# A decoder layer on one core: v's two parts side by side, a mask by select, the embedding's projection inside the mixer, and a new written order

## The chip, the cores and the metric

The kernel runs on 1 core of one Trainium2 chip. The metric is the device time in microseconds (us) of one launch. The engines are PE (TensorE), DVE (VectorE), ACT (ScalarE), POOL (GpSimd) and SP (SyncE, which here issues the transfers). Each takes its instructions strictly in the order in which they were emitted.

## The reference

One decoder layer on x of 512 tokens and 1024 features, in float32:

```python
x = x + 0.5 * swiglu(rmsnorm(x, g1), wgu1, wdown1)          # 1024 -> 2 x 2816 -> 1024
h = rmsnorm(x, g_mix);  z = h @ w_in                        # zq, zk, zv, zc, zg
q, k = rope(rmsnorm(zq)), rope(rmsnorm(zk)); v = zv         # 16 query heads, 2 key heads, 64 wide
a = attention(q, k, v, sinks, window=128, block=128) @ attn_proj
ca, cb = split(zc); u = ca * sigmoid(cb)
c = silu(layernorm(causal_depthwise_conv31(u))) @ conv_proj
ga, gb = split(zg)
x = x + (sigmoid(ga) * a + sigmoid(gb) * c) @ w_out
x = x + 0.5 * swiglu(rmsnorm(x, g2), wgu2, wdown2)
e = rmsnorm(p @ ple_proj, g_ple)                            # p: 512 x 256
x = x + sigmoid(rmsnorm(x, g_gate) @ ple_gate_w) * e
```

A query sees the 128 latest keys, itself included: of the block before it those later than its own place, of its own block those not later.

## The kernel before, in words

Features lie on the 128 partitions and the 512 tokens are the columns, so nearly every product is one of 128x128 by 128x512 into one PSUM bank. Float32 accuracy comes from three products of a reduced type per tile (`mm3`, line 691): a value is split into a high part (a copy by ACT) and a low part (a subtraction by DVE, or by POOL where the name is in `FLEX`), `split_into` (line 664), and high x low, high x high and low x high are added up in PSUM. A weight piece of 128x1024 is loaded and split in the same way, `piece` (line 679): tiles `raw_`, `whi_`, `wlo_`, three buffers each. Other tiles of 128x512 share 53 buffers.

The parts follow each other: the first feed-forward part (`ffn`, line 840: products f_g and f_u for each of 22 columns of the hidden layer, then f_d), the mixer, cp (conv_proj), wo (w_out), the second feed-forward part, the embedding's projection e, the gate pg and the output. In `ffn` the norm is applied behind the product, so products start on x times the gain (h_h, h_l) while the sum of squares (n_sq) is still being made.

The string `ORDER` (line 40) lists the mixer's steps by letter and number: K keys and values, Q queries of one key head group, a and b the convolution's two inputs (products ca, cb), A scores (transposes qTp, products sc), E softmax, V values (`values`, line 1113: transposes pT, products o), g and h the two gates (products ga, gb), p the attention's projection (ap), L the layer norm (ln_). For A, E and V the numbers 0 to 3 are the four blocks of 128 tokens of head group 0, 4 to 7 those of group 1. Channels 0, 2 and 4 of the convolution run on POOL (taps y<-y,ct), the other five on DVE (cz, 31 taps each).

In `values`, for each block of tokens but the first, o of a head group is the sum over both key heads hh of (v of the block before) x (softmax weights p) + (dv, v of this block less that before) x (the weights po, with keys later than the query set to zero by a product with a mask). Both heads go into one bank: the stationary operand is v with 64 zero columns, so that each head reaches its own half of the rows, and each of the 2 or 4 terms takes three products.

`record` writes all steps down as instructions, `simulate` (line 384) places them in time by a table of costs and of free buffers, with `deadlines` (line 357) as priorities, and `hybrid_layer` (line 1288) emits every engine's instructions in the order of the starts found (all through line 1314, hence one line number in every row). PE takes groups of products in the written order, and may take one of the next 8 groups when the first isn't ready.

Of the kernel before, what the change touches and what calls it, by code (L numbers as in the profile page):

```python
# [16 lines left out]
P = 128  # L17
# [5 lines left out]
KF = FF // P  # L23
# [17 lines left out]
K0 a0 a1 Q0 b1 a2 b2 b0 A0 a3 A1 b3 E0 E1 A2 a4 V0 E2 A3 a5 E3 V1 b4 Q1 V2 V3  # L41
b5 A4 g5 a6 A5 E4 A6 V4 E5 a7 b7 A7 g4 V5 g3 h4 E6 V6 E7 g6 g2 V7 b6 g1 g0 p0
p2 L0 h6 h7 g7 h1 p1 p7 h3 p5 p3 h2 p6 h0 p4 h5
"""
POOLCH = (0, 2, 4)
WARM = 9
FLEX = ("wkv", "wq", "wzc", "wzg", "wap")
# [3 lines left out]
class VT:  # L51


    def __init__(self, name, shape, dtype, cls):
        self.name, self.shape, self.dtype, self.cls = name, tuple(shape), dtype, cls
        self.log = []
        self.left = 0
        self.slot = self.real = None
        self.late = False

# [159 lines left out]
class Program:  # L220
# [65 lines left out]
    def costs(self, op, eng=None):  # L286
# [9 lines left out]
        vecs = sum(isinstance(v, V) for v in list(op.a[3:]) + list(op.k.values()))  # L296
# [24 lines left out]
        elif eng == "ACT":  # L321
            op.cost, op.lat = 0.07 + n * 0.88e-3, 0.17
            if vecs:
                op.cost += 0.08
# [32 lines left out]
def deadlines(prog, when):  # L357
# [5 lines left out]
    for op in reversed(prog.ops):  # L363
# [9 lines left out]
        for s in op.succs:  # L373
            d = s.ls
            if s.preds[op] and not s.eng == op.eng == "PE":
                d -= op.lat + (1.8 + op.dma if op.eng == "SP" else 0.0)
            ls = min(ls, d - op.cost)
        op.ls = ls
# [5 lines left out]
def simulate(prog, slots):  # L384

    free = {c: deque(range(n)) for c, n in slots.items()}
    cap = {"cz": 2}
    ncz = 0
# [24 lines left out]
    for op in prog.ops:  # L413
        if op.npred == 0:
            push(0.0, "ready", op)
    push(0.0, "wake")
# [6 lines left out]
    def can(op, slack):  # L423
# [10 lines left out]
        for c, vts in need.items():  # L434
# [7 lines left out]
            if any(vt.name.startswith("cz") for vt in vts) and ncz >= cap["cz"]:  # L442
# [3 lines left out]
    def launch(op, t):  # L446
        nonlocal dma_free, aset, ncz, lock_dve, lock_pool
        for v in op.writes:
            vt = v.vt
            if vt.slot is None:  # L450
                vt.slot = free[vt.cls].popleft()
                if vt.name.startswith("cz"):
                    ncz += 1
# [80 lines left out]
    while left:  # L534
# [4 lines left out]
        while events and events[0][0] <= t + 1e-9:  # L539
            _, _, kind, x = heapq.heappop(events)  # L540
            if kind == "done":
# [8 lines left out]
                for vt in x.vts:  # L550
                    vt.n -= 1
                    if vt.n == 0:
                        free[vt.cls].append(vt.slot)
                        if vt.name.startswith("cz"):
                            ncz -= 1
            elif kind == "ready" and x.eng != "PE":
                insort(ready[x.eng], (x.ls, x.i, x))
        for e in ENGINES:
# [11 lines left out]
            for key, _, op in ready[e]:  # L570
                if best is not None and key >= best[0]:
                    break
                if e == "ACT" and op.fset and op.fset != aset:
# [61 lines left out]
def record():  # L635
# [165 lines left out]
    for k in range(KD):  # L801
        sq = ftile(f"n1_sq{k}")
        nc.scalar.activation(sq, x[k], AF.Square)
# [7 lines left out]
    masks = nc.tile("masks", [P, 2, W], F32, "c")  # L811
# [28 lines left out]
    def ffn(tag, wgu, wdown, h, ss, after, cuts, late):  # L840
# [18 lines left out]

        for i in range(KF):  # L860
            ws = [piece(wgu, 2 * i + kh, cuts=cuts if i == 0 else 1) for kh in range(2)]
            pg, pu = ps_tile(f"{tag}_g{i}"), ps_tile(f"{tag}_u{i}")
            if i == late and late:
                rb = spread(f"{tag}_n", r)
            kn = 2 if i == late else KD
            for k0 in range(0, KD, kn):
                with nc.group(f"{tag}_gu{i}_{k0}"):
                    for k in range(k0, k0 + kn):
                        c = (k % 4) * 256
                        for j, ps in enumerate((pg, pu)):  # L870
                            mm3(
                                ps, part(ws[k // 4], slice(c + j * P, c + (j + 1) * P)), h[k], k == 0, k == KD - 1,
                                0 if cuts > 1 and i == k == 0 else 1,
                            )
# [29 lines left out]
    ffn("f1", "wgu1", "wd1", h, ss, after, 4, 2)  # L904
# [93 lines left out]
    kz = [nc.tile(f"kz{p}", [P, NT, 2, P], F32R, "k") for p in "hl"]  # L998
    for z in kz:
        nc.gpsimd.memset(z.bitcast(F32)[HD:P, :, 0], 0.0)  # L1000
        nc.gpsimd.memset(z.bitcast(F32)[0:HD, :, 1], 0.0)

    vp = [nc.tile(f"v{t}", [P, 2, 3, HD], F32R, "a") for t in range(NT)]

    dv = [nc.tile(f"dv{t}", [P, 2, 3, HD], F32R, "a") if t else None for t in range(NT)]
    vf = nc.tile("vf", [P, NT, NKV, HD], F32, "a")

    def keys_values():
# [3 lines left out]
        for t in range(NT):  # L1012
# [4 lines left out]
            nc.gpsimd.memset(vp[t].bitcast(F32)[:, :, 1], 0.0)  # L1017
# [396 lines left out]
```

## Time and profile before

| | us |
|---|---|
| median of 3 runs (lowest, highest) | 1218.81 (1218.6, 1219.24) |
| the profiled execution | 1218.67 |
| its span in the profile | 1216.8 |
| PE busy | 1201.5 (99%) |
| DVE, ACT, POOL busy | 732.6, 490.2, 332.7 |

PE is the engine that is always at work. The chain of work that ended last lies on PE for 90% of the span. A matmul's row shows 0.39 us, but the products overlap: what one costs is the distance from its start to the next start. "[3.42 <-DVE oT1l L1314]" behind a row says that the engine was idle for 3.42 us before it and that the last thing it waited for was oT1l on DVE. Names in rows of the trace have their numbers taken off: f_g is that of any column.

### The profile page before, as it was taken

To read this page: it belongs to the slowest core of one execution; us is meant where nothing else is said; L and a number is where in the kernel's file an instruction comes from. 1 tells how busy PE (TensorE), PEld (TensorE's weight loads), DVE (VectorE), ACT (ScalarE), POOL (GpSimd) and SP (SyncE) were. 2 spreads that over 40 slices of the span, in tenths; PEclk is the share of its full clock that TensorE was granted. 3 is DMA by queue.
4 is the path that set the end of the run, shared out by engine and by line. 5 is a ranking of instruction groups with operands and counts; after the bars stand their busy time and mean duration, and the time that the engine had idled before them with its cause. 6 is when DMAs were issued, how large, how long until landed. Compare 5 with 4: busy or idle time off the path is not lost.

```text
span 1216.8 us, 14137 instructions
## 1 busy us (share of the span) xinstructions
PE 1201.5 (99%) x5408; PEld 996.7 (82%) x5408; DVE 732.6 (60%) x1019; ACT 490.2 (40%) x780; POOL 332.7 (27%) x345
## 2 busy tenths in 40 slices
PE   9999999999999999998999999999999999999998
PEld 7888888888888887877888888888888888888886
DVE  5644445434446888997898775755444444344466
ACT  5433223222223749769573463333233232222251
POOL 2000000001112798996897200510000000022230
PEclk9999999999999999999999999999999999999999
DMA  7232222333332231212122323232322323333321
GB/s 239 87 104 89 102 99 92 100 91 99 96 100 90 86 103 53 72 51 70 64 91 89 101 91 113 95 104 87 104 91 100 101 90 100 92 98 97 100 87 70
DMA packets 35203, 115.11 MB, mean 95 GB/s; under 512 B 4416, under 2 KB 6080, under 8 KB 35136
## 3 DMA queue, kind: packets, MB, share of 16 engines
q1 hardware_dynamic: 34992, 114.18, 28.9%
q8 instruction: 42, 0.69, 0.2%
q14 instruction: 25, 0.20, 0.1%
q10 hardware_dynamic: 144, 0.03, 0.0%
HBM read 112.10 MB, written 2.10 MB: 94 GB/s over the span
## 4 chain that ended last, share of the span: by engine, by line
PE 90%; ACT 5%; DVE 3%; issue 1%; DMA 0%; SPq 0%; DVEq 0%
PE f_d L1314 20%; PE f_g L1314 19%; PE f_u L1314 19%; PE pg L1314 4%; PE ap L1314 4%; PE wo L1314 4%; PE cp L1314 4%; PE gb L1314 3%; ACT s L1314 3%; PE ga L1314 3%; PE ca L1314 3%; PE cb L1314 3%; PE q0b L1314 2%; DVE cz L1314 1%; PE kvb L1314 1%; PE e L1314 1%
## 5 line engine op out<-in xcount | busy, mean ns | idle before, releaser
L1314 ACT ACTIVATE whi_wgu<-raw_wgu 128x1024 fp32r<-128x1024 f32 (+1 forms) x94 | 94.5, 1005 | 254.3 <-PE f_u L1314 233.4
L1314 DVE TENSOR_TENSOR wlo_wgu<-raw_wgu,whi_wgu 128x1024 fp32r<-128x1024 f32 (+1 forms) x94 | 110.3, 1175 | 108.3 <-ACT whi_wgu L1314 108.3
L1314 DVE TENSOR_TENSOR wlo_wd<-raw_wd,whi_wd 128x1024 fp32r<-128x1024 f32 (+1 forms) x48 | 65.7, 1369 | 102.2 <-ACT whi_wd L1314 102.2
L1314 ACT ACTIVATE whi_wd<-raw_wd 128x1024 fp32r<-128x1024 f32 (+1 forms) x48 | 47.5, 990 | 177.1 <-PE f_d L1314 107.6
L1314 POOL TENSOR_TENSOR y<-y,ct 128x511 f32<-128x511 f32 (+28 forms) x90 | 113.8, 1285 | 4.8 <-DVE y L1314 3.0
L1314 POOL TENSOR_TENSOR pg_ss_sq<-x 128x512 f32<-128x512 f32 x8 | 8.3, 1039 | 338.1 <-DVE x L1314 324.1
L1314 DVE SCALAR_TENSOR_TENSOR cz<-u,dww,cz 128x504 f32<-128x504 f32 (+24 forms) x145 | 100.0, 728 | 0.8
L1314 POOL TENSOR_TENSOR mix_ss_sq<-x 128x512 f32<-128x512 f32 x8 | 8.3, 1040 | 328.7 <-DVE x L1314 328.7
L1314 PE MATMUL f_d<-f_a_h,wlo_wd 128*128 128x512 f32 x224 | 87.1, 389 | 0.0
L1314 PE MATMUL f_d<-f_a_h,whi_wd 128*128 128x512 f32 x224 | 87.1, 389 | 0.0
L1314 PE MATMUL f_d<-f_a_l,whi_wd 128*128 128x512 f32 x224 | 87.1, 389 | 0.0
L1314 DVE TENSOR_TENSOR f_gs<-f_g,f_n_rb 128x512 f32<-128x512 f32 x44 | 30.3, 691 | 94.1 <-PE f_g L1314 92.6
L1314 PE MATMUL f_g<-h_h,wlo_wgu 128*128 128x512 f32 x176 | 69.0, 392 | 1.0 <-DVE wlo_wgu L1314 0.9
L1314 PE MATMUL f_g<-h_h,whi_wgu 128*128 128x512 f32 x176 | 68.9, 391 | 0.0
L1314 PE MATMUL f_g<-h_l,whi_wgu 128*128 128x512 f32 x176 | 68.6, 390 | 0.0
L1314 PE MATMUL f_g<-f_h_h,wlo_wgu 128*128 128x512 f32 x176 | 68.6, 390 | 0.0
L1314 PE MATMUL f_u<-h_h,wlo_wgu 128*128 128x512 f32 x176 | 68.5, 389 | 0.0
L1314 PE MATMUL f_u<-h_h,whi_wgu 128*128 128x512 f32 x176 | 68.5, 389 | 0.0
L1314 PE MATMUL f_g<-f_h_l,whi_wgu 128*128 128x512 f32 x176 | 68.5, 389 | 0.0
L1314 PE MATMUL f_u<-f_h_h,wlo_wgu 128*128 128x512 f32 x176 | 68.5, 389 | 0.0
L1314 PE MATMUL f_g<-f_h_h,whi_wgu 128*128 128x512 f32 x176 | 68.5, 389 | 0.0
L1314 PE MATMUL f_u<-h_l,whi_wgu 128*128 128x512 f32 x176 | 68.5, 389 | 0.0
(407 smaller groups left out, 3163.2 us busy)
## 6 DMA issues: line engine op xcount, KB each, us to landing
raw_wgu<-in_wgu SPq DMA_DIRECT2D x86, 512.0 KB, 3.5
raw_wd<-in_wd SPq DMA_DIRECT2D x32, 512.0 KB, 3.5
raw_wzc<-in_wzc SPq DMA_DIRECT2D x16, 512.0 KB, 3.5
raw_wzg<-in_wzg SPq DMA_DIRECT2D x16, 512.0 KB, 3.5
raw_wd<-in_wd SPq DMA_DIRECT2D x16, 384.0 KB, 3.1
raw_wq<-in_wq SPq DMA_DIRECT2D x8, 512.0 KB, 3.4
raw_wap<-in_wap SPq DMA_DIRECT2D x8, 512.0 KB, 3.5
raw_wcp<-in_wcp SPq DMA_DIRECT2D x8, 512.0 KB, 3.5
```

Of the source, the lines that this page charges most:

```text
L1314: getattr(engines[op.eng], op.what)(*a, **k)
```

## The change

1. `values`: the stationary operand is [v_hi | v_lo], 64 columns each, so one product gives both halves of p_h x v. Each term takes two products (p_h, p_l) and each head has a bank of its own; ACT copies the half that came from the low part to SBUF (`of`) and DVE adds the two halves.
2. The weights of the own block come from a select on POOL (`affine_select`) on p_h and p_l instead of a product with a mask on DVE or POOL.
3. The squares for the norms of queries and keys move from POOL to ACT. kz is laid out by head; seven memsets of v and dv go, and their splits are made for each head apart.
4. The embedding's projection (8 x 6 products, its norm) is a step "e" of the mixer. Its eight results are kept through the second feed-forward part.
5. `ffn`: the first two columns of the first part are computed side by side (loop over the 8 feature tiles outside, over the two columns inside), with the weights of both in four cuts. The squares for its norm start no earlier than 14.0 on the planner's clock. In the second part the first column is one group of 48 products rather than four.
6. The planner: a limit of four `ct` tiles, another price of vector operands on ACT, and a new `ORDER`.

```diff
 ORDER = """
-K0 a0 a1 Q0 b1 a2 b2 b0 A0 a3 A1 b3 E0 E1 A2 a4 V0 E2 A3 a5 E3 V1 b4 Q1 V2 V3
...
+K0 a0 a2 a1 Q0 A0 b2 b1 b0 a3 A1 E0 E1 b3 A2 E2 a4 V0 A3 a5 E3 V1 b4 Q1 V2 b5
...
+g1 p0 p2 g7 L0 p3 p6 p4 h3 p7 p5 p1 e0 h5 h6 e1 h0 h2
 """
...
+        sq.vt.after = 14.0
         nc.scalar.activation(sq, x[k], AF.Square)
...
-    masks = nc.tile("masks", [P, 2, W], F32, "c")
+    masks = nc.tile("masks", [P, W], F32, "c")
...
+        def products(i, ks):
+            if i not in gu:
+                gu[i] = ps_tile(f"{tag}_g{i}"), ps_tile(f"{tag}_u{i}")
+            for k in ks:
+                if k % 4 == 0:
+                    ws[i] = piece(wgu, 2 * i + k // 4, cuts=cuts if i < late else 1)
...
+                for j, ps in enumerate(gu[i]):
+                    mm3(
+                        ps, part(ws[i], slice(c + j * P, c + (j + 1) * P)), h[k], k == 0, k == KD - 1,
+                        0 if cuts > 1 and i == k == 0 else 1,
+                    )
+        for k in range(KD if late else 0):
+            for i in range(late):
+                products(i, [k])
         for i in range(KF):
-            ws = [piece(wgu, 2 * i + kh, cuts=cuts if i == 0 else 1) for kh in range(2)]
...
-            nc.gpsimd.tensor_tensor(sq, z3, z3, op=ALU.mult)
+            nc.scalar.activation(sq, z3, AF.Square)
...
             for o, p in zip(po, pr):
-                nc.flex.tensor_tensor(
-                    o.rearrange("p (j k) -> p j k", j=4), p.bitcast(F32).rearrange("p (j k) -> p j k", j=4), own,
-                    op=ALU.mult,
+                nc.gpsimd.affine_select(
+                    o, p.bitcast(F32), pattern=[[0, 4], [1, W]], compare_op=ALU.is_ge, fill=0.0,
+                    base=0, channel_multiplier=-1,
                 )
             parts.append((hh, dv[t], po))
-        po = ps_tile(f"o{g}_{t}")
-        with nc.group(f"o{g}_{t}"):
-            for n, (hh, v, pr) in enumerate(parts):
-                vv = [v[:, i, hh : hh + 2].rearrange("p a d -> p (a d)") for i in range(2)]
-                mm3(po, vv, pr, n == 0, n == len(parts) - 1)
+        of = ftile(f"of{g}_{t}")
+        for hh in range(2):
+            po = ps_tile(f"o{g}_{t}_{hh}")
+            mine = [(v, pr) for h, v, pr in parts if h == hh]
+            with nc.group(f"o{g}_{t}_{hh}"):
+                for n, (v, pr) in enumerate(mine):
+                    vv = v[:, hh].rearrange("p a d -> p (a d)")
+                    nc.tensor.matmul(po, vv, pr[0], start=n == 0, stop=False)
+                    nc.tensor.matmul(po, vv, pr[1], start=False, stop=n == len(mine) - 1)
+            r, other = (slice(h * HD, (h + 1) * HD) for h in (hh, 1 - hh))
+            nc.scalar.copy(of[r], po[other])
+            nc.vector.tensor_tensor(of[r], po[r], of[r], op=ALU.add)
         to = [o[:, :, t * P : (t + 1) * P] for o in oq[g]]
-        split_into(to[0], to[1], po.rearrange("p (j k) -> p j k", j=4))
+        split_into(to[0], to[1], of.rearrange("p (j k) -> p j k", j=4))
...
+    def embedding(i):
...
+        w = piece("wple", i)
+        for j in range(4):
...
+                    mm3(ps, part(w, slice(c, c + P)), pin[k], k == 0, k == KP - 1)
+            e = ftile(f"es{n}")
+            nc.scalar.copy(e, ps)
+            es.append(e)
+            sse.add(ps, on_act=True)
+        if len(es) == KD:
+            rbe = spread("ple", mean_rstd("ple", sse.accs, D))
```

Three places show how the instructions stand. First, SP at the program's start, before and then after; raw_wgu10 is the first weight piece of column 0, raw_wgu12 that of column 1, x0 to x3 are tiles of the input.

```order
L1314 DMA x0_70<-in_xT 128x512
L1314 DMA raw_wgu10_78<-in_wgu1 128x256
L1314 DMA x1_83<-in_xT 128x512
L1314 DMA raw_wgu10_78<-in_wgu1 128x256
L1314 DMA x2_98<-in_xT 128x512
L1314 DMA raw_wgu10_78<-in_wgu1 128x256
L1314 DMA x3_104<-in_xT 128x512
L1314 DMA raw_wgu10_78<-in_wgu1 128x256
L1314 DMA x4_112<-in_xT 128x512
```

```order
L1346 DMA x0_70<-in_xT 128x512
L1346 DMA raw_wgu10_78<-in_wgu1 128x256
L1346 DMA raw_wgu12_83<-in_wgu1 128x256
L1346 DMA x1_89<-in_xT 128x512
L1346 DMA raw_wgu10_78<-in_wgu1 128x256
L1346 DMA raw_wgu12_83<-in_wgu1 128x256
L1346 DMA x2_104<-in_xT 128x512
L1346 DMA raw_wgu10_78<-in_wgu1 128x256
L1346 DMA raw_wgu12_83<-in_wgu1 128x256
```

Between two tiles of x there is now a cut of column 1 beside that of column 0.

Second, PE where the scores of head group 1 begin, before and then after; sc1_1_3 is the last score product of block 1 of that group, qTp1_2 the transposes of the queries of block 2, ga5 an attention gate.

```order
L1314 MATMUL sc1_0_3_4262<-kzh_72,qT1_0_l_4199 128x256
L1314 MATMUL sc1_0_3_4262<-kzh_72,qT1_0_h_4184 128x256
L1314 MATMUL sc1_0_3_4262<-kzl_101,qT1_0_h_4184 128x256
L1314 MATMUL qTp1_1_4272<-ident_74,zq1_1_4053 128x128 x4
L1314 MATMUL qTp1_2_4289<-ident_74,zq1_2_4061 128x128 x4
L1314 MATMUL sc1_1_0_4307<-kzh_72,qT1_1_l_4300 128x512
L1314 MATMUL sc1_1_0_4307<-kzh_72,qT1_1_h_4284 128x512
L1314 MATMUL sc1_1_0_4307<-kzl_101,qT1_1_h_4284 128x512
```

```order
L1346 MATMUL sc1_1_3_4308<-kzh_72,qT1_1_l_4199 128x512
L1346 MATMUL sc1_1_3_4308<-kzh_72,qT1_1_h_4184 128x512
L1346 MATMUL sc1_1_3_4308<-kzl_101,qT1_1_h_4184 128x512
L1346 MATMUL qTp1_2_4317<-ident_74,zq1_2_4115 128x128 x4
L1346 MATMUL ga5_4323<-mix_h0_h_1946,wlo_wzg10_4207 128x512
L1346 MATMUL ga5_4323<-mix_h0_h_1946,whi_wzg10_4190 128x512
L1346 MATMUL ga5_4323<-mix_h0_l_1966,whi_wzg10_4190 128x512
```

Before, the transposes of two blocks and the scores that read them stand behind each other. After, a gate's 24 products stand behind the transposes of block 2.

Third, PE around the transposes of the softmax weights of group 1, before and then after; pT1_1_0 belongs to block 1 and key head 0, o1_2_0 is the values' product of block 2 and key head 0, cb6 the convolution's gate of channel 6.

```order
L1314 MATMUL pT1_1_0_4750<-ident_74,s1_1_0_4316 128x128 x2
L1314 MATMUL pT1_1_0_4750<-ident_74,s1_1_1_4334 128x128 x2
L1314 MATMUL pT1_1_1_4759<-ident_74,s1_1_0_4316 128x128 x2
L1314 MATMUL pT1_1_1_4759<-ident_74,s1_1_1_4334 128x128 x2
L1314 MATMUL pT1_2_0_4766<-ident_74,s1_2_0_4354 128x128 x2
L1314 MATMUL pT1_2_0_4766<-ident_74,s1_2_1_4370 128x128 x2
L1314 MATMUL pT1_2_1_4774<-ident_74,s1_2_0_4354 128x128 x2
L1314 MATMUL pT1_2_1_4774<-ident_74,s1_2_1_4370 128x128 x2
L1314 MATMUL ga6_4787<-mix_h0_h_1940,wlo_wzg12_4684 128x512
```

```order
L1346 MATMUL o1_2_0_4712<-p1_2_0_h_4656,v1_2772 128x512
L1346 MATMUL o1_2_0_4712<-p1_2_0_l_4666,v1_2772 128x512
L1346 MATMUL o1_2_0_4712<-po1_2_0h_4683,v2_2779 128x512
L1346 MATMUL o1_2_0_4712<-po1_2_0l_4692,v2_2779 128x512
L1346 MATMUL pT1_1_0_4726<-ident_74,s1_1_0_4290 128x128 x2
L1346 MATMUL pT1_1_0_4726<-ident_74,s1_1_1_4312 128x128 x2
L1346 MATMUL cb6_4734<-mix_h0_h_1946,wlo_wzc13_4660 128x512
L1346 MATMUL cb6_4734<-mix_h0_h_1946,whi_wzc13_4644 128x512
L1346 MATMUL cb6_4734<-mix_h0_l_1966,whi_wzc13_4644 128x512
```

Before, the transposes of two blocks stand together ahead of ga6. After, two of them at a time stand between products of the convolution's inputs and of the values.

## Rows read from the trace of the kernel before

**Rows 1.** The first part of the page: the span, and of each engine the busy time, its share of the span and its instructions.

```profile
span 1216.8 us, 14137 instructions
PE 1201.5 (99%) x5408; PEld 996.7 (82%) x5408; DVE 732.6 (60%) x1019; ACT 490.2 (40%) x780; POOL 332.7 (27%) x345
```

**Rows 2.** The timeline of PE in the first up-projections, one row per product of 128x512: start, duration, engine, line, operation and tiles; the rows left out are 41 more products.

```profile
19.64 0.39 PE L1314 MATMUL f_u<-h_l,whi_wgu 128*128 128x512 f32 x1
...
29.16 0.39 PE L1314 MATMUL f_u<-h_l,whi_wgu 128*128 128x512 f32 x1
```

**Rows 3.** The view of the waits of PE over the span, by the tile that waited and the one waited for: us in total, times, longest.

```profile
PE ga L1314 <- DVE oT1l L1314: 3.4, 1, 3.4
PE sc L1314 <- DVE qT_l L1314: 1.6, 1, 1.6
PE qTp L1314 <- DVE s L1314: 1.1, 1, 1.1
PE f_g L1314 <- DVE wlo_wgu L1314: 0.9, 1, 0.9
```

**Rows 4.** The view by windows of 20 us: the window, its length, then PE, PEld, DVE, ACT and POOL busy with their instructions, PE's granted clock, the DMA share and GB/s.

```profile
460.00:480.00 20.00, 19.23 (x94) 15.68 (x94) 16.59 (x32) 19.99 (x71) 16.30 (x29) 1.00 0.08 27
...
520.00:540.00 20.00, 17.24 (x86) 14.27 (x85) 19.72 (x36) 12.75 (x24) 19.27 (x25) 1.00 0.16 53
...
560.00:580.00 20.00, 16.57 (x80) 13.69 (x79) 15.79 (x30) 19.97 (x67) 12.64 (x26) 0.90 0.24 75
580.00:600.00 20.00, 20.00 (x88) 16.50 (x87) 16.75 (x25) 11.13 (x20) 15.98 (x15) 0.93 0.17 56
...
640.00:660.00 20.00, 20.00 (x90) 16.57 (x89) 19.97 (x30) 6.04 (x9) 18.73 (x14) 1.00 0.23 79
```

**Rows 5.** The timeline of PE around the longest wait.

```profile
571.76 1.94 PE L1314 MATMUL pT<-ident,s 128*128 128x128 f32 x16
577.12 0.79 PE L1314 MATMUL ga<-mix_h_h,wlo_wzg 128*128 128x512 f32 x1 [3.42 <-DVE oT1l L1314]
577.71 0.63 PE L1314 MATMUL ga<-mix_h_h,whi_wzg 128*128 128x512 f32 x1
...
582.41 0.58 PE L1314 MATMUL ga<-mix_h_h,wlo_wzg 128*128 128x512 f32 x1
```

**Rows 6.** The timeline of PE and ACT at the start; the product at 8.20 is the seventh, that at 19.64 in Rows 2 the 54th.

```profile
3.42 0.63 ACT L1314 ACTIVATE n_sq<-x 128x512 f32<-128x512 f32 x1 [0.97 <-DMA x<-in_xT]
5.02 0.79 PE L1314 MATMUL f_g<-h_h,whi_wgu 128*128 128x512 f32 x1
...
6.30 0.73 ACT L1314 ACTIVATE h_h<-x,g_all 128x512 fp32r<-128x512 f32 x1 [1.34 <-DMA x<-in_xT]
...
8.20 0.50 PE L1314 MATMUL f_g<-h_h,wlo_wgu 128*128 128x512 f32 x1 [0.92 <-DVE wlo_wgu L1314]
```

**Rows 7.** The groups of PE by line and form, the values' product of v and the high part of the weights: busy us, mean ns of one, idle before.

```profile
L1314 PE MATMUL o<-p_h,v 128*128 128x512 f32 x32 | 9.9, 392 | 0.0
```

**Rows 8.** The groups of DVE by line and form: the low half of a weight piece in the feed-forward parts and in attn_proj, a mask product of values(), a low half of the attention output, a convolution tap.

```profile
L1314 DVE TENSOR_TENSOR wlo_wgu<-raw_wgu,whi_wgu 128x1024 fp32r<-128x1024 f32 x86 | 107.1, 1245 | 108.3 <-ACT whi_wgu L1314 108.3
L1314 DVE TENSOR_TENSOR wlo_wap<-raw_wap,whi_wap 128x1024 fp32r<-128x1024 f32 x6 | 10.8, 1797 | 0.4 <-ACT whi_wap L1314 0.4
L1314 DVE TENSOR_TENSOR po_1l<-p_l,masks 128x512 fp32r<-128x512 f32 x4 | 4.7, 1178 | 0.0
L1314 DVE TENSOR_TENSOR oT1l<-o,oT1h 128x512 fp32r<-128x512 f32 x4 | 2.7, 680 | 1.6 <-ACT oT1h L1314 1.6
L1314 DVE SCALAR_TENSOR_TENSOR cz<-u,dww,cz 128x498 f32<-128x498 f32 x5 | 3.6, 730 | 0.0
```

**Rows 9.** The groups of ACT by line and form: a square of 128x512, and a copy of 128x512 from PSUM.

```profile
L1314 ACT ACTIVATE ln_v_sq<-y 128x512 f32<-128x512 f32 x8 | 4.8, 633 | 0.2 <-DVE y L1314 0.2
L1314 ACT COPY mix_n_rb<-mix_n_sp 128x512 f32<-128x512 f32 x1 | 0.6, 567 | 0.0
```

**Rows 10.** The groups of POOL by line and form: a square of the queries, mask products, and the one select.

```profile
L1314 POOL TENSOR_TENSOR q_sq<-zq 128x512 f32<-128x512 f32 x8 | 9.7, 1215 | 0.0
L1314 POOL TENSOR_TENSOR po_1h<-p_h,masks 128x512 fp32r<-128x512 f32 x4 | 7.0, 1762 | 0.0
L1314 POOL TENSOR_TENSOR po_0h<-p_h,masks 128x512 fp32r<-128x512 f32 x5 | 6.9, 1377 | 1.5 <-PE o L1314 1.5
L1314 POOL TENSOR_SCALAR_AFFINE_SELECT ident<-ident 128x128 f32<-128x128 f32 x1 | 0.3, 286 | 0.0
```

**Rows 11.** The timeline of DVE and PE at the layer norm: the last tap, the low half of the channel sum, and the first product that reads it.

```profile
656.56 0.74 DVE L1314 SCALAR_TENSOR_TENSOR y<-u,dww,cz 128x511 f32<-128x511 f32 x1
...
665.91 0.68 DVE L1314 TENSOR_TENSOR ln_s_l<-ln_acc,ln_s_h 128x512 fp32r<-128x512 f32 x1
...
670.54 0.39 PE L1314 MATMUL ln_mb<-ln_s_h,mean_r 128*128 128x512 f32 x1
```

**Rows 12.** The timeline of PE and DVE where the second feed-forward part ends: its last product, the embedding's first, and the last low half of the gate's input.

```profile
1153.19 0.39 PE L1314 MATMUL f_d<-f_a_l,whi_wd 128*128 128x512 f32 x1
...
1153.42 0.39 PE L1314 MATMUL e<-pin_h,wlo_wple 128*128 128x512 f32 x1
...
1156.43 1.78 DVE L1314 SCALAR_TENSOR_TENSOR pg_h_l<-x,g_all,pg_h_h 128x512 fp32r<-128x512 f32 x1
```

More of the change, by code (lines that the diff above doesn't have):

```diff
@@ L57, in __init__ @@
         self.left = 0
+        self.after = 0.0
         self.slot = self.real = None
         self.late = False
+        self.kind = name[:2] if name[:2] in CAPS else None
 _SHADOW, _REGION = {}, {}
@@ L295, in costs @@
         op.dma = 0.0
-        vecs = sum(isinstance(v, V) for v in list(op.a[3:]) + list(op.k.values()))
+        vecs = sum(isinstance(v, V) for v in [*op.a[3:], *(v for n, v in op.k.items() if n != "accum_out")])
         if eng == "PE":
@@ L415, in simulate @@
             push(0.0, "ready", op)
+        if op.outs and op.outs[0].after:
+            push(op.outs[0].after, "wake")
     push(0.0, "wake")
@@ L441, in can @@
                 return False
-            if any(vt.name.startswith("cz") for vt in vts) and ncz >= cap["cz"]:
+            if any(vt.kind and inuse[vt.kind] >= CAPS[vt.kind] for vt in vts):
                 return False
@@ L572, in simulate @@
                     break
+                if op.outs and op.outs[0].after > t:
+                    continue
                 if e == "ACT" and op.fset and op.fset != aset:
@@ L858, in gated @@
             return split(f"{tag}_a{i}", u)
+        ws, gu = {}, {}
+        def products(i, ks):
[4 more added lines that the diff above has]
+                    ws[i] = piece(wgu, 2 * i + k // 4, cuts=cuts if i < late else 1)
+                if k == ks[0]:
+                    cm = nc.group(f"{tag}_gu{i}_{k}")
+                    cm.__enter__()
+                c = (k % 4) * 256
+                for j, ps in enumerate(gu[i]):
[3 more added lines that the diff above has]
+                    )
+            cm.__exit__(None, None, None)
+        for k in range(KD if late else 0):
+            for i in range(late):
+                products(i, [k])
         for i in range(KF):
-            ws = [piece(wgu, 2 * i + kh, cuts=cuts if i == 0 else 1) for kh in range(2)]
-            pg, pu = ps_tile(f"{tag}_g{i}"), ps_tile(f"{tag}_u{i}")
             if i == late and late:
                 rb = spread(f"{tag}_n", r)
[L865 to L874, printed above, removed]
+            if i >= late:
+                kn = 2 if i == late and late else KD
+                for k0 in range(0, KD, kn):
+                    products(i, range(k0, k0 + kn))
+            pg, pu = gu[i]
             if i == max(0, late - 1):
@@ L1052, in record @@
     state = {}
[L1054 removed]
+    later = masks.unsqueeze(1).broadcast_to([P, 2, W])
     def scores(g, t):
```

121 lines of the change are left out of this document (55 added, 66 removed).

## The prediction

> **What bounds the kernel now.** I read the first part of the page first: PE is busy for 1201.5 of the span's 1216.8 us [rows 1]. So a product taken off PE is worth the distance between two products, and all else that can be won is waits of PE. The distance is read off the timeline: 42 distances between 19.64 and 29.16, 9.52/42 = 0.2267 us [rows 2]; the 0.39 shown is a duration that overlaps the next. The view of PE's waits then names what it waits for: 3.4 us, 1.6 and 1.1 in the mixer, 0.9 at the start [rows 3]. The windows say where and who was full there: PE lacks 0.77 us in 460 to 480 (ACT 19.99 of 20), 2.76 in 520 to 540 (DVE 19.72) and 3.43 in 560 to 580 (ACT 19.97) [rows 4], together 6.96. Behind the last one the windows show a granted clock of 0.90 and 0.93, and the timeline shows why that counts: after the 3.42 us in which PE stood still, products came 0.59 and then 11 times (582.41 - 577.71)/11 = 0.427 us apart, which is 512 columns at the lower clock level of 1.2 GHz [rows 5]. That cost (0.59 - 0.23) + 11 x (0.427 - 0.227) = 2.6. The mixer loses 9.5 us in all.
>
> At the start the product at 5.02 is the first and that at 19.64 the 54th: 14.62 us where 53 distances are 12.0, so 2.6 lost. The first square stands on ACT from 3.42, for 0.63, ahead of the first h; the seventh product waits until 8.20, since the second tile of x landed only for an ACT operation at 6.30 [rows 6].
>
> **The change, part by part.** The sum is made against the profiled execution, 1218.67 us, of which 1.87 lie around the span; it stands 0.14 under the median of the runs.
>
> *Values.* Over the eight blocks there are 28 terms (two heads, one weight set in the first block of a group, two in the three others: 2 groups x 2 x (1 + 3 x 2) = 28). Each took three products and takes two. The view by form shows the product with v's halves at 392 ns, no other than the rest [rows 7], and it streams 512 columns in either form, so 28 x 0.2267 = 6.35 us go: **-6.35**. The Trainium skill, TensorE: Matmul & The Clock Gate, section Back-to-back issue gap, gives some 131 ns per product of 512 columns in a stream of weight loads and products; by that the term would be 3.7, an estimate, and the sum 2.7 higher. The trace contradicts it with 0.2267 over 42 distances.
>
> What the values add lies elsewhere: 16 copies on ACT and 16 additions on DVE, each on 64 partitions by 512 columns, against ten mask products that leave DVE. On DVE 16 x 0.68 = 10.9 come and 10 x 1.178 = 11.8 go [rows 8]: nothing. On ACT 16 x 0.567 = 9.1 come, and the 8 squares of the queries, 8 x 0.633 = 5.1 [rows 9]. Both lie beside PE's work except where ACT is full (460 to 480 and 560 to 580); queued behind them there are the softmax's exponentials, on which the transposes pT wait. If that cover is gone it shows as waits below. On POOL 14 mask products (mean of 1.762 and 1.377, 1.57) and 8 squares of 1.215 go, 31.7 us, and 24 selects come [rows 10]. The trace has one select, of a quarter of the columns, at 0.286: that is the lower end, the slowest mask product, 1.762, the upper; I take four times the select seen, 1.14, since it is the only row of that operation: 27.4. So POOL comes out some 4 us lighter (24.8 lighter to 10.6 heavier at the ends).
>
> *Start.* SP now issues a cut of column 1 beside each of column 0, so 12 products stand behind every tile of x instead of 6: 2.7 us of work per tile, where the trace shows 1.4 to have been too little. The second tile of x comes one issue and one cut later, but 12 products cover that. The square that no longer stands ahead of the first h gives up to 0.5 more. Of the 2.6 lost I take 2.0 as won: **-2.0** (bounds 0, if the transfers only shift, and -2.6).
>
> *The new order in the mixer.* The three waits were looked up in the new order. The 1.6 us came from scores right behind the transposes that they read; now a gate's 24 products, 5.4 us, stand between. The 3.4 us and the low clock came from 16 transposes ahead of ga6, with banks that had still to be emptied; now the transposes are spread between products. Waits remain where a group stands close behind what it reads: the first values' product of block 0 and the transposes of group 1's queries behind the second query projection, 0 to 1.5 each, I take 0.75 each; cp0, 0 to 1, 0.5. At the layer norm PE has 240 products = 54.4 us between the last gate of the convolution and ln_mb. DVE has there, by the new order, 44 taps x 0.73 = 32.1, 14 operations x 0.68 = 9.5 and 8 low halves of 1.245 to 1.797 = 10.0 to 14.4, plus 1 us of the chain around them: 52.6 to 57. Before there were 4 us to spare, 665.91 + 0.68 to 670.54 [rows 11]. So a wait of 0 to 2.6 is new there; I take 1.5. And 1.3, the mean of the two lesser waits seen, for a place that I overlook. Together 4.8 in place of 9.5: **-4.7** (bounds: all gone, -9.5; or +5, one more wait like the longest with the low clock behind it, and the ln_mb one in full).
>
> *Embedding and tail.* Its 48 products, 10.9 us, only move. They covered the end of the second feed-forward part: the last product there began at 1153.19, the last low half of the gate's input was ready at 1156.43 + 1.78 = 1158.21 [rows 12]. Now pg0 begins at 1153.42, and the products that need that half are its last three: 1153.42 + 21 x 0.2267 = 1158.18. So the cover just holds: **0** (bounds 0 and +1.8, one more such DVE operation in the way). The eight results held through the second part leave fewer free buffers, and the splits of its last columns come later; four columns' banks, 10.9 us each, cover that: 0 (to +1).
>
> Sum: -6.35 - 2.0 - 4.7 + 0 = -13.05, so 1218.67 - 13.05 = **1205.6 us**. All at the good ends: 1218.67 - 6.35 - 2.6 - 9.5 = 1200.2.
>
> **The rivals.**
> *The waits only move.* Each head's values take a bank of their own and the chain from product to oT is longer by a copy and an addition (0.57 + 0.68), with ACT fuller by 14 us in a stage where it was full twice. For it: both long waits before were of this kind. Against it: the new order puts products between. Then 9.5 stay: 1218.67 - 6.35 - 2.0 = 1210.3.
> *Nearly no waits.* If the order fits the chip as well as it does in the second feed-forward part, of which the rows of waits name nothing: about 1200.5. Against it: DVE's 52.6 to 57 against 54.4.
> *Slower: POOL comes late to the layer norm.* POOL is 18.7 of 20 busy in 640 to 660 and holds three channels of the convolution, whose sum ln_mb reads; PE takes its instructions in order, so all behind ln_mb waits with it. At c us per select the lag is 24 x c - 31.7 - 4: it decides from c = 2.0 on, where it is 12.3, the low clock adds 2.6, and the gain is gone. With c = 2.15 the lag is 15.9, the time 1205.6 - 1.5 + 15.9 + 2.6 = 1222.6. For it: no row has a select of this size. Against it: it reads one operand, where the mask products with two took 1.762 at most. The Trainium skill, SBUF — State Buffer, section Who interferes with whom, says that a GpSimd instruction reading SBUF and a DVE instruction with two inputs there shut each other out for the whole instruction; that speaks for this case, as all 24 are now on POOL. The trace agrees in part: the same low half took 1.797 in the mixer and 1.245 elsewhere, a delay of 0.55, less than one POOL operation, and 22 mask products and squares were there before.
>
> **How the numbers follow.** Chances: the forecast 0.63 (its own range 1202 to 1208.5), the waits only move 0.22 (1208.5 to 1212), nearly none 0.08 (1200 to 1202), slower or level through POOL 0.07. The range 1200 to 1212 leaves out that last case and a little of the second. A change of under 0.2%, 2.4 us, can't be told from none here. Faster: 0.93; of the POOL case 0.03 falls within 0.2% and 0.04 above.
>
> **What would show it.** PE's matmuls 28 fewer at the same 0.2267 distance; at the start a 54th product some 2 us nearer to the first and no wait of f_g for wlo_wgu; no window of the mixer with PE under 18 and a clock under 1; a wait at ln_mb of up to 2.6, and no idle time ahead of pg. Wrong would be: a select above 1.8 us, a wait at ln_mb above 5, an ACT that is full with PE idle around the transposes of group 1, or PE waiting in the second feed-forward part.

## The result and the profile after

The changed kernel takes 1205.02 us (median; single runs 1203.2 to 1205.14) against 1218.82 of the kernel before, a ratio of 0.9883 with the interval 0.9866 to 0.99. It is 13.8 us faster; the forecast was 1205.6. The total was right, and two of its terms were not, in opposite directions, which is luck as far as the total goes.

The profiled execution took 1205.14 us. The first part of its page, beside [rows 1]:

```profile
span 1203.4 us, 14206 instructions
PE 1193.8 (99%) x5380; PEld 990.4 (82%) x5380; DVE 729.6 (61%) x1034; ACT 506.7 (42%) x821; POOL 319.4 (27%) x340
```

PE has 28 matmuls fewer and is as full as before. ACT has 16.5 us more to do, POOL 13.3 less.

The view of PE's waits of the changed kernel (us in total, times, longest), beside [rows 3]:

```profile
PE ca L1346 <- DVE of L1346: 1.1, 1, 1.1
PE f_g L1346 <- ACT whi_wgu L1346: 0.6, 1, 0.6
PE sc L1346 <- DVE of L1346: 0.3, 1, 0.3
```

The waits of 3.4, 1.6 and 1.1 us are gone. Two new ones, 1.1 and 0.3, stand behind `of`, the tile of the added copy and addition. The wait at the start is there still, for another engine.

Windows of 20 us of the changed kernel, with the columns of [rows 4]:

```profile
460.00:480.00 20.00, 20.00 (x98) 16.16 (x97) 19.34 (x38) 19.90 (x63) 14.80 (x29) 1.00 0.12 34
500.00:520.00 20.00, 18.91 (x96) 15.86 (x95) 19.94 (x28) 12.93 (x21) 16.88 (x26) 1.00 0.21 68
520.00:540.00 20.00, 19.60 (x89) 15.60 (x88) 19.77 (x47) 16.73 (x31) 18.58 (x15) 1.00 0.18 64
560.00:580.00 20.00, 19.87 (x96) 16.26 (x95) 17.08 (x27) 19.06 (x44) 15.33 (x28) 1.00 0.21 72
```

PE lacks 1.09 + 0.40 + 0.13 = 1.6 us in the mixer, and the granted clock is 1.00 in every window of it. Before it was 6.96 of idle time by the forecast's three windows (the one from 500 to 520 lacked another 0.23) and 2.6 of low clock. That is 7.9 us won; the forecast had 4.7. The distance from the 54th product to the first one of the second feed-forward part says the same without windows; that first product, before and after:

```profile
792.97 0.39 PE L1314 MATMUL f_g<-f_h_h,wlo_wgu 128*128 128x512 f32 x1
...
791.72 0.39 PE L1346 MATMUL f_g<-f_h_h,wlo_wgu 128*128 128x512 f32 x1
```

With the 54th product at 19.64 and 20.42 (below) these are 773.33 and 771.30 us. The changed kernel has 6.35 us of products less there, and the embedding more, by which its tail is 12.1 us shorter (1216.8 - 1153.19 against 1203.4 - 1151.94). So the waits fell by 773.33 - 6.35 + 12.1 - 771.30 = 7.8 us.

The start, on ACT and PE, with the 54th product as the last row, beside [rows 2, 6]; the first two rows (L1314) are from the kernel before:

```profile
1.17 1.28 ACT L1314 ACT_TABLE_LOAD   x1 [1.17 <-PEq L1403]
...
3.95 0.70 ACT L1314 ACTIVATE h_h<-x,g_all 128x512 fp32r<-128x512 f32 x1
...
3.59 1.28 ACT L1346 ACT_TABLE_LOAD   x1 [3.59 <-DMA x<-in_xT]
4.88 0.72 ACT L1346 ACTIVATE h_h<-x,g_all 128x512 fp32r<-128x512 f32 x1
...
5.96 0.79 PE L1346 MATMUL f_g<-h_h,whi_wgu 128*128 128x512 f32 x1 [0.65 <-ACT whi_wgu L1346]
...
7.80 0.63 PE L1346 MATMUL f_u<-h_h,whi_wgu 128*128 128x512 f32 x1
8.23 0.63 PE L1346 MATMUL f_u<-h_h,wlo_wgu 128*128 128x512 f32 x1
...
20.42 0.39 PE L1346 MATMUL f_u<-h_l,whi_wgu 128*128 128x512 f32 x1
```

The first product comes at 5.96 (5.02 before), seven of the next ones 0.43 apart, and the 54th at 20.42 (19.64 before): in this execution the start lost 0.78 us where 2.0 were to be won. The rows of the load say why. The load of ACT's table, 1.28 us, waited for no transfer before and began at 1.17; now it ended its idle time on the transfer of x, stands behind that transfer, and the first h behind the load.

The layer norm and the end of the second feed-forward part, in the timelines of ACT, DVE and PE, beside [rows 11, 12]:

```profile
659.44 0.68 DVE L1346 TENSOR_TENSOR ln_s_l<-ln_acc,ln_s_h 128x512 fp32r<-128x512 f32 x1
...
662.44 0.39 PE L1346 MATMUL ln_mb<-ln_s_h,mean_r 128*128 128x512 f32 x1
...
1151.94 0.39 PE L1346 MATMUL f_d<-f_a_l,whi_wd 128*128 128x512 f32 x1
1152.17 0.39 PE L1346 MATMUL pg<-pg_h_h,wlo_wgate 128*128 128x512 f32 x1
1155.19 1.77 DVE L1346 SCALAR_TENSOR_TENSOR pg_h_l<-x,g_all,pg_h_h 128x512 fp32r<-128x512 f32 x1
...
1157.38 0.39 PE L1346 MATMUL pg<-pg_h_l,whi_wgate 128*128 128x512 f32 x1
```

ln_mb's input was ready at 660.12, 2.3 us ahead of it: no wait. The gate's first product follows the last one of f_d at 0.23; the last low half was ready at 1156.96, 0.4 ahead of the product that reads it, the gate's 24th.

The groups by form of the operations that are new, on POOL, ACT and DVE:

```profile
L1346 POOL TENSOR_SCALAR_AFFINE_SELECT po_0h<-p_h 128x512 fp32r<-128x512 f32 x6 | 4.8, 800 | 4.1 <-ACT p_h L1346 3.9 <-PE o L1346 0.2
L1346 POOL TENSOR_SCALAR_AFFINE_SELECT po_1l<-p_l 128x512 fp32r<-128x512 f32 x6 | 3.8, 634 | 1.7 <-DVE oT1l L1346 1.7
...
L1346 ACT COPY of<-o 64x512 f32<-64x512 f32 x16 | 9.2, 582 | 1.2 <-PE o L1346 0.8
...
L1346 DVE TENSOR_TENSOR of<-o,of 64x512 f32<-64x512 f32 x16 | 10.8, 684 | 3.0 <-ACT of L1346 2.8
```

A select of 128x512 takes 0.63 to 0.80 us in the mean of a form, where 1.14 was assumed; copy and addition cost what the rows of before gave.

The terms now add up: products -6.35, start +0.78, waits of the mixer -7.9, tail 0; together -13.5, and the two profiled executions lie 1218.67 - 1205.14 = 13.53 apart.

### The profile page after: what moved, and what is told of

Read it like the earlier page. It is cut to its first block, busy times and chain, and to the rows that moved or that the text cites. A ratio compares the mean times of both kernels' runs of the same rounds, so it can differ in the third digit from the quotient of the medians.

```text
span 1203.4 us, 14206 instructions
## 1 busy us (share of the span) xinstructions
PE 1193.8 (99%) x5380; PEld 990.4 (82%) x5380; DVE 729.6 (61%) x1034; ACT 506.7 (42%) x821; POOL 319.4 (27%) x340
## 4 chain that ended last, share of the span: by engine, by line
PE 96%; DVE 3%; issue 0%; ACT 0%; DMA 0%; POOL 0%; DVEq 0%; ACTq 0%; POOLq 0%
PE f_g L1346 20%; PE f_u L1346 20%; PE f_d L1346 20%; PE gb L1346 4%; PE cb L1346 4%; PE pg L1346 4%; PE wo L1346 4%; PE ap L1346 4%; PE cp L1346 4%; PE ca L1346 3%; PE ga L1346 3%; PE q0b L1346 2%; PE sc L1346 1%; DVE cz L1346 1%; PE kvb L1346 1%; PE e L1346 1%
## 5 line engine op out<-in xcount | busy, mean ns | idle before, releaser
L1346 POOL TENSOR_TENSOR y<-y,ct 128x509 f32<-128x509 f32 (+28 forms) x90 | 114.9, 1297 | 6.8 <-ACT ct L1346 5.1
L1346 DVE SCALAR_TENSOR_TENSOR cz<-u,dww,cz 128x504 f32<-128x504 f32 (+26 forms) x145 | 103.9, 731 | 1.7
```

The costliest lines, as they stand in the source:

```text
L1346: getattr(engines[op.eng], op.what)(*a, **k)
```

## The experiments

Two questions were open: what made the start slower, and what removed the waits. Two theories answered the second: the written order (the forecast's reason), or the new form of the values with the selects and the squares on ACT. Most edits make the planner lay out all instructions anew, so that a part undone shows its own price and that of another plan; the last two runs hold the plan fixed. A median also holds the clock at the start, which differs from one execution to the next by 1.6 us (last section); where that matters, the distance from the 54th product to the first one of the second feed-forward part, 771.30 us in the changed kernel, is given beside it. In three profiled executions with the changed kernel's mixer (the changed kernel twice, and with the load early) it agrees within 0.3 us. Times are medians; the kernel before ran beside each set at 1218.7 to 1220.7.

**The changed kernel again**, as it is.

> The changed kernel once more, beside the three that follow. Both theories: 1205.0, with single runs between 1203.2 and 1205.2 as before.

1204.98 us (1203.52 to 1205.1). Of eight runs in all, six lie at 1204.9 to 1205.2 and two near 1203.4.

**The table load early.**

```diff
     nc.vector.memset(ones, 1.0)
+    early = small("early", 1)
+    nc.scalar.activation(early, ones[:, 0:1], AF.Square)
```

> The changed kernel, and one square of a single column of ones put first on ACT, which needs no transfer. Theory (the table load): in the changed kernel the first instruction of ACT waits for x and for the gains, and the load of ACT's table (1.28 us) took over the wait for x, so that it stands behind the transfer instead of beside it; PE ran out of warm-up products, and its clock fell. With the load early the first product comes about 1.3 us sooner, near 4.7, and none at 0.427: 2.0 to 3.5 us less, 1201.5 to 1203.0. Rival (the transfers): the extra cuts between the tiles of x set the start; 1204.6 to 1205.2.

1202.89 us (1202.82 to 1203.14): 2.1 less than the changed kernel beside it. ACT and PE at the start, the last row again the 54th product:

```profile
1.23 1.28 ACT L1348 ACT_TABLE_LOAD   x1 [1.23 <-PEq L1437]
...
3.80 0.72 ACT L1348 ACTIVATE h_h<-x,g_all 128x512 fp32r<-128x512 f32 x1 [1.07 <-DMA g_all<-in_gains]
...
4.88 0.49 PE L1348 MATMUL f_g<-h_h,whi_wgu 128*128 128x512 f32 x1
...
18.15 0.39 PE L1348 MATMUL f_u<-h_l,whi_wgu 128*128 128x512 f32 x1
```

The load runs beside the transfers, the first product comes at 4.88 instead of 5.96, and the 54th at 18.15 instead of 20.42. The theory of the table load holds for the late first product, 1.08 us of it; the transfers alone don't explain it. The larger part of the 2.27 us at the 54th product goes with the clock, and not as the theory had it: it did not fall in the changed kernel's profiled execution. By the trace's records of the granted clock it stood at the lower of its two levels (1.2 GHz) until 10.4 us there, and here it was at the upper level (2.4 GHz) from 4.0 us on. This version is faster than both kernels: 0.9866 of the kernel before (0.9852 to 0.9881).

**One column after the other**, with the load late, and then with the load early too.

```diff
-        for k in range(KD if late else 0):
-            for i in range(late):
+        for i in range(late):
+            for k in range(KD):
                 products(i, [k])
...
-                    ws[i] = piece(wgu, 2 * i + k // 4, cuts=cuts if i < late else 1)
+                    ws[i] = piece(wgu, 2 * i + k // 4, cuts=cuts if i == 0 else 1)
```

> The changed kernel, but the first two columns one after the other, with cuts for the first alone, as in the kernel before; the table load stays late. Theory (the table load): the first product is still at 5.6 to 6.0 and waits for x tiles come back: 1205 to 1206. Rival (the transfers): the start of the kernel before comes back, 1203.5 to 1204.3.

1203.71 us (1203.2 to 1204.97): a miss for the theory, which had 1205 to 1206, and inside the rival's range. PE at its start:

```profile
6.04 0.50 PE L1346 MATMUL f_g<-h_h,whi_wgu 128*128 128x512 f32 x1 [0.72 <-ACT whi_wgu L1346]
...
7.19 0.39 PE L1346 MATMUL f_g<-h_l,whi_wgu 128*128 128x512 f32 x1
7.42 0.40 PE L1346 MATMUL f_u<-h_h,whi_wgu 128*128 128x512 f32 x1
...
19.27 0.39 PE L1346 MATMUL f_u<-h_l,whi_wgu 128*128 128x512 f32 x1
```

The first product is as late as the theory says, 6.04. What the theory didn't foresee: the clock was granted in full from 5.8 us on here, and from the third product on they come some 0.23 apart.

> The changed kernel with the first two columns one after the other and the early square. Theory (the table load): the start of the kernel before without the square ahead of the first h, 0.75 + 0.5 less than the changed kernel: 1203.4 to 1204.2, and some 1 us behind the run with the early square alone, which is what the columns side by side are worth. Rival (the transfers): no faster than one by one without the early square, and not slower than the early square alone.

1203.52 us (1203.32 to 1204.24), as expected: first product at 4.97, 54th at 19.01. So the two columns side by side are worth 19.01 - 18.15 = 0.86 us when the load is early, 0.6 by the medians, and the forecast's idea of them was right in kind. Against the run before, the early load alone is worth 19.27 - 19.01 = 0.26 us when the columns come one after the other, 0.2 by the medians.

**The old order in the changed kernel**, and **the new order in the kernel before.**

```diff
-K0 a0 a2 a1 Q0 A0 b2 b1 b0 a3 A1 E0 E1 b3 A2 E2 a4 V0 A3 a5 E3 V1 b4 Q1 V2 b5
...
+K0 a0 a1 Q0 b1 a2 b2 b0 A0 a3 A1 b3 E0 E1 A2 a4 V0 E2 A3 a5 E3 V1 b4 Q1 V2 V3
...
+p2 L0 h6 h7 g7 h1 p1 p7 h3 p5 p3 h2 p6 e0 h0 p4 e1 h5
```

> The changed kernel with the written order of the kernel before; the embedding's two steps stand between its last ones. Theory (the order removed the waits): PE's long waits in the scores and ahead of ga6 come back, at least 5 of the 7.9 us: 1210 or more. Rival (the new form of the values, with the selects and the squares on ACT, removed them): 1207 at most.

1207.93 us (1207.8 to 1209.27), 2.9 more than the changed kernel: between the two. The median understates it, since the clock was full from 4.9 us on in the profiled execution of this run, and its 54th product came 1.55 us sooner than the changed kernel's. That product, the first one of the second feed-forward part, and PE's longest wait in the mixer:

```profile
18.87 0.39 PE L1346 MATMUL f_u<-h_l,whi_wgu 128*128 128x512 f32 x1
...
794.70 0.39 PE L1346 MATMUL f_g<-f_h_h,wlo_wgu 128*128 128x512 f32 x1
```

```profile
PE sc L1346 <- DVE qT_l L1346: 1.7, 1, 1.7
```

The distance is 775.83, 4.5 more than the 771.30 of the changed kernel. The wait in the scores is back, the one ahead of ga6 is not. So of the 7.8 us of waits 4.5 come back with the old order: short of the theory's 5, and far from nothing.

> The kernel before with the new written order, without the embedding's steps. Theory (the order removed the waits): 5 to 8 us less, 1210.8 to 1213.8. Rival (it needs the new form of the values): 1216 or more.

1231.39 us (1223.51 to 1239.5), ratio 1.0084 (1.005 to 1.0118): slower than before. Neither theory had that. PE's waits in its profiled execution, of 1224.37 us:

```profile
PE ga L1314 <- DVE oT1l L1314: 3.1, 1, 3.1
PE o L1314 <- DVE p_l L1314: 2.3, 1, 2.3
PE sc L1314 <- DVE qT_l L1314: 1.6, 1, 1.6
...
PE qTp L1314 <- DVE s L1314: 1.2, 1, 1.2
```

The longest waits of the kernel before are all there, and a new one of the values' products o. The order without the other parts removes nothing; in the mixer of this execution PE took 6.2 us longer than in the kernel before. Together: all other parts of the change under the old order are worth 12 us (1220.0 beside it; 10.9 by the two profiled executions), 6.35 of it in products and 7.8 - 4.5 = 3.3 in waits of the mixer; the order on top of them takes the other 4.5; and the order alone costs. So neither theory holds alone: the order pays only together with the rest. Which parts of the rest it needs is not settled by these two runs, since the planner's new limits, the layout of the keys and the embedding in the mixer go with the form of the values here.

**The old values.** Zero columns beside v, three products per term, one bank, as in the kernel before; the selects stay.

```diff
-                    vv = v[:, hh].rearrange("p a d -> p (a d)")
-                    nc.tensor.matmul(po, vv, pr[0], start=n == 0, stop=False)
-                    nc.tensor.matmul(po, vv, pr[1], start=False, stop=n == len(mine) - 1)
+                vv = [v[:, i, hh : hh + 2].rearrange("p a d -> p (a d)") for i in range(2)]
+                mm3(po, vv, pr, n == 0, n == len(parts) - 1)
```

> The changed kernel with the values' products of the kernel before: v with zero columns, three products per term, one bank; the selects stay. 28 products more. Theory (a product costs its distance of 0.2267): 6.35 more, 1211.0 to 1211.8. Rival (it costs less beside others, or the waits move): 1208.7 or less, or 1214 or more.

1214.09 us (1212.46 to 1216.0), 9.1 more than the changed kernel: 6.35 is the price of 28 products, and the 2.8 left over are put down to waits. The longest one in the mixer:

```profile
PE o L1340 <- POOL po_1l L1340: 2.6, 1, 2.6
```

The rival's second half (1214 or more, the waits move) has it, by a hair.

**The product with a mask**, new plan.

```diff
-                nc.gpsimd.affine_select(
-                    o, p.bitcast(F32), pattern=[[0, 4], [1, W]], compare_op=ALU.is_ge, fill=0.0,
-                    base=0, channel_multiplier=-1,
+                nc.flex.tensor_tensor(
+                    o.rearrange("p (j k) -> p j k", j=4), p.bitcast(F32).rearrange("p (j k) -> p j k", j=4), own,
+                    op=ALU.mult,
                 )
```

> The changed kernel with the own block's weights made by the product with a mask, on DVE or POOL as the planner chooses, instead of the select. Theory (POOL and DVE have room): hidden, 1205 to 1206.5. Rival (the select, at 0.63 to 0.80 us where a product took 1.18 to 1.76, is what took the waits of the values away): 1207.5 or more.

1207.56 us (1206.43 to 1208.63), 2.6 more. The bound of the rival is 1207.5, so this alone decides nothing.

**The squares on POOL**, new plan.

```diff
-            nc.scalar.activation(sq, z3, AF.Square)
+            nc.gpsimd.tensor_tensor(sq, z3, z3, op=ALU.mult)
```

> The changed kernel with the squares of queries and keys on POOL again. Theory (the order removed the waits): within 1 us of the changed kernel, 1204.3 to 1206. Rival (POOL was what the chain of the queries waited for): 1207 or more.

1216.07 us (1215.26 to 1217.17), 11 more: far beyond what the theory allowed. The timeline of PE, ACT and DVE at its longest wait:

```profile
461.73 0.60 PE L1346 MATMUL qTp<-ident,zq 128*128 128x128 f32 x4
463.56 0.19 ACT L1346 ACTIVATE es<-es 128x8 f32<-128x8 f32 x1
463.91 0.59 ACT L1346 ACTIVATE qT_h<-qTp 128x512 fp32r<-128x512 f32 x1
466.22 0.69 DVE L1346 TENSOR_TENSOR qT_l<-qTp,qT_h 128x512 fp32r<-128x512 f32 x1
466.96 0.50 PE L1346 MATMUL sc<-kzh,qT_l 128*128 128x512 f32 x1 [4.64 <-DVE qT_l L1346]
```

In this plan qT_h stands on ACT behind the eight exponentials of a softmax, qT_l on DVE behind five taps of the convolution, and the scores right behind their transposes. No square is in this chain; the plan is.

**The embedding back in the tail**, new plan.

```diff
-g1 p0 p2 g7 L0 p3 p6 p4 h3 p7 p5 p1 e0 h5 h6 e1 h0 h2
+g1 p0 p2 g7 L0 p3 p6 p4 h3 p7 p5 p1 h5 h6 h0 h2
...
     rb4 = None
+    embedding(0)
+    rb4 = spread("pg", mean_rstd("pg", ss4.accs, D))
+    embedding(1)
```

> The changed kernel with the embedding's products and norm back between the second feed-forward part and the gate. Theory (they only move): 1204.5 to 1205.5. Rival (in the mixer they cover a wait, at the layer norm above all): 1207 or more.

1210.6 us (1210.01 to 1210.84), 5.6 more. The two longest waits of the mixer in this plan, neither of them in the changed kernel:

```profile
PE sc L1347 <- DVE qT_l L1347: 3.0, 1, 3.0
...
PE cp L1347 <- ACT cv_h L1347: 0.5, 1, 0.5
```

The first lies at 514 us, 150 us ahead of where the embedding stood in the changed kernel. The second, between the layer norm and the end of cp, lies behind the place where the embedding's products had stood as cover, and the row shows less than it costs, since cp's products also come up to 0.5 us apart around it. The first and the last of its 192 products:

```profile
694.13 0.40 PE L1347 MATMUL cp<-cv_h,wlo_wcp 128*128 128x512 f32 x1
...
740.97 0.39 PE L1347 MATMUL cp<-cv_l,whi_wcp 128*128 128x512 f32 x1
```

That is 46.84 us where 191 distances of 0.2267 are 43.30: 3.5 us of the 5.6, at the place that the rival named. In the kernel before, cp ran at full pace without this cover, so the loss goes with the new order or with this plan of it.

**The squares on POOL in the same plan.** The changed kernel's order on every engine; only the squares are emitted for POOL, in their places.

```diff
+            if op.what == "activation" and name[:5] in ("q0_sq", "q1_sq", "k_sq0", "k_sq1", "k_sq2", "k_sq3"):
+                nc.gpsimd.tensor_tensor(a[0], a[1], a[1], op=ALU.mult)
+                continue
             getattr(engines[op.eng], op.what)(*a, **k)
```

> The changed kernel with its own order of instructions on every engine; only the squares of queries and keys are computed by POOL, in the same places, instead of ACT. No new plan is made, unlike in the run with the squares on POOL. Theory (the loss of that run came from the new plan that the edit set off, the squares themselves are hidden): 1204.5 to 1206.5. Rival (the squares on POOL delay the queries): 1210 or more.

1209.71 us (1208.69 to 1209.95), 4.7 more, between the two and near to the rival. The profiled execution had its 54th product at 18.78 and the first one of the second feed-forward part at 796.54, a distance of 777.76, 6.5 more than the changed kernel's. So of the 11 us with a new plan the squares are 4.7 to 6.5, and the rest is the plan. PE's waits:

```profile
PE qTp L1350 <- POOL zq L1350: 1.7, 1, 1.7
PE qTp L1350 <- DVE u L1350: 1.4, 1, 1.4
```

Transposes wait for the queries zq, whose rotation stands on POOL behind the squares.

**The mask product on POOL in the same plan.**

```diff
+            if op.what == "affine_select" and op.outs[0].name.startswith("po"):
+                nc.gpsimd.tensor_tensor(
+                    a[0].rearrange("p (j k) -> p j k", j=4), a[1].rearrange("p (j k) -> p j k", j=4), own3, op=ALU.mult
+                )
+                continue
             getattr(engines[op.eng], op.what)(*a, **k)
```

> The changed kernel with its own order of instructions; each of the 24 selects is replaced, in its place on POOL, by a product with a mask made once at the start. At 1.4 to 1.8 us instead of 0.63 to 0.80 POOL has about 20 us more to do in the mixer. Theory (POOL has that room, and what the run with mask products lost came from its new plan): 1204.5 to 1206.5. Rival (the short select is what keeps the values' products from waiting, and POOL in time for the layer norm): 1208 or more.

1211.17 us (1211.15 to 1211.46), 6.2 more: the rival. One of the forms on POOL, and waits that follow:

```profile
L1353 POOL TENSOR_TENSOR po_1l<-p_l,own 128x512 fp32r<-128x512 f32 x6 | 8.8, 1459 | 0.0
```

```profile
PE pT L1357 <- POOL s L1357: 1.6, 3, 0.8
```

24 products of 1.29 to 1.52 us take twice the time of the selects, and what stands behind them on POOL, the scaling of the softmax weights s, comes late to the transposes pT. The short select is worth these 6 us in this plan. At the layer norm there is no wait in this run either. The prices of this run and the one before add up to more than the 7.8 us of waits that the whole change removed: each is what one part is worth in a plan that was made for both, and they must not be added.

## Why the prediction was right, and where it was not

*Values: right.* PE's distance is the same 0.2267, and undoing this part cost 9.1 us, the 6.35 and more, though in a new plan. The 56 products of the changed kernel take 13.80 us, each counted to the next start on PE, the 84 before 19.67: 5.9 less; the missing 0.5 are short waits among them. The 131 ns per product that the Trainium skill, TensorE: Matmul & The Clock Gate, section Back-to-back issue gap, gives would have made it 3.7, an estimate; that fits neither.

*Start: too much forecast, and wrong in sign in the profiled execution.* The step that failed is "The square that no longer stands ahead of the first h gives up to 0.5 more", and with it the table load, which the sum put at nothing. The square had been hardly a burden: with it the first h began at 3.95, without it and with the load early at 3.80. But the table load stood ahead of it, waited for nothing and ran beside the transfer. With the square moved, the first instruction of ACT was h_h, which waits for two transfers, and the load in front of it took over the wait for x. That put the first product at 5.96 instead of 4.88, 1.08 us later. With the load early the start won 19.64 - 18.15 = 1.5 of the 2.0 forecast, 0.9 of it by the two columns side by side. With the load late the 54th product came at 18.78 to 18.91 in executions with a full clock from the first product on, 0.8 sooner than before, and at 20.29 to 20.57 in the others. So of the 20.42 - 18.15 = 2.27 us some 0.7 are the load alone and some 1.6 the clock; that the late load makes the low clock likelier fits all runs, but is not shown.

*Waits of the mixer: right in sign, too small, and for half of the reason.* Forecast were 4.8 left of 9.5; 1.6 were left. The step that failed is "The three waits were looked up in the new order": it took the order alone to remove them. In the kernel before, the new order left all three (3.1, 1.6 and 1.2) and cost 6.2 us in the mixer; under the old order the other parts of the change removed 3.3 of the 7.8 us, and only on top of them did the order remove 4.5. With the plan held fixed the short selects carry 6.2 us and the squares on ACT 4.7 to 6.5, so the plan that this order led to rests on both. What mis-sized the term, as far as the rows show: a select was priced at 1.14 and took 0.63 to 0.80, so that the 24 came to 16.2 us instead of 27.4 and POOL out 13.3 us lighter, not 4; and the low halves of attn_proj took 1.33 us on DVE, near the lower end of the forecast's 1.245 to 1.797, so that ln_mb did not wait at all. The embedding was put at nothing in the mixer, and may have removed some of these waits too: without it cp lost 3.5 us.

*Embedding and tail: right for the tail.* No wait ahead of pg, and 0.4 us to spare where the forecast saw none: it let the gate's last three products wait for the last low half, and only the 24th reads it, 23 distances behind the first. That the products "only move" is not the whole of it, as the run with the embedding back in the tail shows.

*The rivals.* "The waits only move" needed ACT's extra copies to be in the way; ACT is at 19.90 in 460 to 480 and PE loses nothing there. Its mechanism is there in small: the two waits left, 1.1 and 0.3, are for `of`, the end of the longer chain, 1.4 of the 9.5. "POOL comes late to the layer norm" did not happen: the selects were short, and even with mask products in their places, when the kernel loses 6.2 us through POOL, the loss lies ahead of the softmax transposes, not at the layer norm. "Nearly no waits" was the nearest in the mixer (its own terms sum to 1200.8, not 1200.5); the start hid it in the total. A right total from two errors of -3.2 and +2.8 us is not a right reading.

What stays open: how much of each undone part is its own price where the plan was made anew (old values, old order, embedding), since no run held the plan fixed for these; and the planner's own changes, the limit of `ct` tiles and the new price on ACT, which no run undid.

## What to carry to other kernels

Before moving the first instruction of an engine, look at which waits it has: a table load in front of it may inherit one, and a load that cost nothing put the first product 1.1 us later here. Where a planner orders everything, undo a part with the order held fixed, by swapping instructions in place, before naming its price; a new plan alone moved the time by some 5 to 6 us here. Try an order of instructions together with the forms it was made for: the same order cost 6.2 us in the mixer without them and won 4.5 with them. And a faster operation on an engine that is 27% busy over the span (POOL, at 14.8 to 18.6 of 20 us in the windows of the mixer shown above) can be worth 6 us when it stands in the chain that PE waits for.

## What the runs showed that was not expected

At which level PE's clock stands at the start was not the same in all executions. Ten profiled executions had the late first product, at 5.96 to 6.17, PE having stood idle for 0.6 to 1.2 us before it. In five of them six or seven products 0.43 us apart followed, and the 54th came at 20.29 to 20.57; in the other five none followed and it came at 18.78 to 18.91 with the columns side by side (19.27 one after the other). The traces' records of the granted clock show two ways to it. In three of the five, both profiles of the changed kernel among them, the clock was at its lower level (1.2 GHz) from the launch until 10.0 to 10.7 us. In the other two it had risen at 4.2 and 4.4, while PE made its warm-up products, and fell again at 7.6 and 7.8; PE had stood idle for 1.2 us before its first product, at 6.0 and 6.2. In the five without slow products it rose at 4.9 to 5.9 and stayed. The view by windows shows 1.00 at the start of the three, since the time ahead of the first record counts there as full.

The difference, some 1.6 us, is the gap between the two groups of runs of the changed kernel (1203.2 and 1203.52 against 1204.94 to 1205.14); that these two runs had a full clock from their first product on is likely, but they were not profiled. With the load early the four runs lie within 0.32 us. In the same way the kernel before, with its stalls in the mixer, spread from 1215.88 (mean granted clock 0.998) to 1221.26 (0.994) beside the experiments, and the new order in that kernel from 1223.51 (0.998) to 1239.5 (0.989).
